# A decoder layer on one core: room for the gates' sources, scalings two by two, sums of down weights placed anew

## The chip, the cores and the metric

The kernel runs on one core of a Trainium2 chip. The metric is the device time of one execution in microseconds (us). Engines: PE (TensorE, matmuls), DVE (VectorE), ACT (ScalarE), POOL (GpSimd) and SP (SyncE, which only issues DMAs here).

## The reference, cut to what matters

One layer of a decoder with 2048 prompt tokens and 64 sample tokens (2112 in all), width 1024, in float32:

```python
h = rms_norm(x, pre_mix_g)
q, k, v, sg_u, sg_v, mq, gate_logits = split(h @ w_in)
# three branches of width 512: window attention, spatial gating, attention into 256 memory rows
sg = u * (tril(sg_w) @ layer_norm(gelu(sg_v)) + sg_b)        # u = gelu(sg_u)
gates = sigmoid(gate_logits)                                 # 3 x 1024 columns
mixed = sum over branches n of gates[n] * (branch[n] @ w_o[n])
x = x + rms_norm(mixed, post_mix_g)
up = rms_norm(x, pre_ffn_g) @ w_up                           # 5632 columns
c = conv_b + three shifted rows of up * conv_w               # causal convolution along tokens
act = gelu(gate half of c) * value half of c                 # 2816 columns
x = x + rms_norm(act @ w_down, post_ffn_g)
```

Outputs are x for prompt and sample tokens, and the caches (keys, values, memory keys and values, the layer-normed sg_v of the samples, the last rows of up).

## The kernel before, in words

Everything is transposed: features on the 128 partitions, tokens along the free axis. A float32 product is made of three passes (`PASSES`): each operand is split into a high part (a cast on ACT, L76) and a low part (a subtraction on DVE, L77), and high by high, high by low and low by high are added in PSUM.

Stage 1 walks over pairs of 128-token blocks. Its first pass (`pass_a`) makes queries, keys, values and both attentions; its weights are five units, `w_a`. Its second pass (`pass_b`) makes the spatial gating with four units, `w_b` (products sv and up, the masked product into psg at L732, then the bias L736 and the product by uT at L737, which gives the branch rows ob, stored at L739). Units are tiles of the pool `w1` (five tiles of 16 KB a partition), loaded in halves through the staging pool `st1` (`load_w1`). Beside them stand `h1`, `st1`, `live1` (values that live through a pair: scores, qT, vg, uT) and `small`. The second pass also prepares sums for the up weights with f < 14: `prep_sums` loads four blocks of a weight, forms four sums or differences on DVE, splits each and stores it to `sum_d`; its tiles are in `raw1b` (5) and `wo1b` (2), on the right side of SBUF.

Stage 2 takes the tokens in three groups of T2 = 704 (two chunks of CW = 352). Its first phase makes the gates (12 weight blocks), its third the up product (22 blocks f), both by one level of Strassen's scheme: a job is one block for one group, seven products of 12 matmuls with sums of the weights (`weights`, L821 raw loads, L847 loads of prepared sums) and sums of the activations (`operands`: load L778, scaling by gain and row norm L780, differences L790, seven sets of four operand tiles). The gates' x and their differences are in the pool `ldg` on the right side (eight tiles of x, one of the norm, four half tiles of differences, 11 × T2 × 4 bytes), the raw weights in `rawg`, next to it. `p5`, `u2` and the like are copies of PSUM tiles on ACT (L891); the sums of products are evicted on DVE (`Sink.add`).

The mix phase takes each group through the three branches n and four blocks op of w_o. A step (n, op) has two tiles o of 24 matmuls (L1023); each is multiplied by its gate (L1032 for n = 0, which makes m; L1035 for the others, then added on POOL, L1036). When a group is done, its rows m, with the sum of their squares, are held, and `post_mix` of the held group runs inside the next group, after the step (n, op) = (0, 1): the row norm, then for each of the eight tiles o a load of x, a scaling of m (L1000, DVE), the addition of x (L1003, POOL), the store of x1 and its square. The last group has no next group in the mix; `late` does the same for it in the up phase, one tile at a time after the blocks f = 2 to 9 of group 0.

In the up phase the jobs are written in the order of g and f. After the blocks f = 3, 7, 11, 15, 19 of group 0 and 3, 7, 11 of group 1 stands a `prep_sums` for one of the eight down weights, d0 to d7. After f = 14 stands `norms`, the row norm of the next group; the next group's operands follow the last block. The up and down phases share a ring of weight tiles, `wof`, with 11 tiles.

The down phase works with two Strassen blocks b and a plain remainder for each group; `final` then scales a group's eight tiles y (L1306), adds x1 (L1310, loaded at L1304 into two tiles) and stores them (L1311). Groups 0 and 1 do that inside the next group's first products; the next group's first product is copied into a y tile at L1229, and such a tile is free when its old y has been stored. In the last group the two chunks are finished one after the other, and in the very last one the odd tiles are added on POOL.

The program is not executed in the order in which it is written. A planner places each engine's instructions, in the order of the program among those that it takes to be ready at that time by its own costs. On the engine the order is then fixed. A pool's tile may lie where an earlier, closed pool's tiles lay (`reuse_waits="tile"`); then its first write waits for the last use of just those tiles that it overlaps. SP issues all loads and stores in one queue.

Of the kernel before, what the change touches and what calls it, by code (L numbers as in the profile page):

```python
# [15 lines left out]
P = 128  # L16
# [114 lines left out]
def stage1(tc, I, O, br, rbc_d, mhalf, gains, split, PASSES, rstd_rows, ident, ident_r, prep_sums, sum_d):  # L131
    nc = tc.nc
    PSUM = bass.MemoryType.PSUM
    with ExitStack() as c1:
        wp = c1.enter_context(tc.tile_pool(name="w1", bufs=5))
        hp = c1.enter_context(tc.tile_pool(name="h1", bufs=3))
        st = c1.enter_context(tc.tile_pool(name="st1", bufs=3))
        lv = c1.enter_context(tc.tile_pool(name="live1", bufs=2))
        small = c1.enter_context(tc.tile_pool(name="small", bufs=2))
        ps_mm = c1.enter_context(tc.tile_pool(name="ps_mm", bufs=3, space=PSUM))  # L140
        ps_o = c1.enter_context(tc.tile_pool(name="ps_o", bufs=1, space=PSUM))
        ps_tr = c1.enter_context(tc.tile_pool(name="ps_tr", bufs=2, space=PSUM))

        def load_w1(u, stage=None, before=None):
            w = wp.tile([P, 2, KT * 256], F32R, tag="w", name=f"w1_{u}")
            for i in range(2):
                if before:
                    before(i)
                t = stage(f"ws_{u}_{i}") if stage else st.tile([P, 1024], F32, tag="st", name=f"ws_{u}_{i}")
                nc.sync.dma_start(out=t, in_=I["w1"][u][:, i * 1024 : (i + 1) * 1024])  # L150
                split(w[:, 0, i * 1024 : (i + 1) * 1024], w[:, 1, i * 1024 : (i + 1) * 1024], t)
            return w
# [97 lines left out]
        sample = ("s", NP, NS, None)  # L250
        with ExitStack() as c2:
            kc = c2.enter_context(tc.tile_pool(name="const1", bufs=1, side="right"))
            wk = c2.enter_context(tc.tile_pool(name="work1", bufs=2, side="right"))
            pass_a(pairs[:2] + [sample] + pairs[2:], dict(locals()))
        with ExitStack() as c2:
            wk = c2.enter_context(tc.tile_pool(name="work1b", bufs=2, reuse_waits="tile"))
            rw = c2.enter_context(tc.tile_pool(name="raw1b", bufs=5, side="right", reuse_waits="tile"))
            wo = c2.enter_context(tc.tile_pool(name="wo1b", bufs=2, side="right", reuse_waits="tile"))
            pass_b(pairs[:1] + [sample] + pairs[1:], dict(locals()))


def pass_a(items, a):
# [41 lines left out]
    rb_mem, r_mem = rstd_of(x_mem, NMEM, "mem")  # L304
    w_a = [load_w1(4 + u, stage) for u in range(5)]
    band = kload("band", [P, 256])
# [597 lines left out]
def gate_phase(c2, tc, env):  # L904
# [4 lines left out]
    lp, rw = pool(c2, "ldg", 1, "right"), pool(c2, "rawg", 11, "right")  # L909
    cp, gp = pool(c2, "cpg", 7), pool(c2, "sg", 4)  # L910
    op_ = {n: pool(c2, "g" + n, 4) for n in ("t4", "b21", "t1", "b11", "t3", "b22", "t2")}
    wo = pool(c2, "wog", 12)
    eng = Strassen(ps2, op_, wo, rw, cp, lp)
# [33 lines left out]
def mix_phase(c2, tc, env):  # L947
# [11 lines left out]
    spare.tile([P, 3456], F32, tag="spare", name="spare")  # L959
    bc, sp, wp, gp, me = (pool(c2, nm, n) for nm, n in (("bc", 4), ("s2", 2), ("w2", 3), ("sg2", 5), ("mxe", 8)))  # L960
    hp = ba, bb, bc
# [26 lines left out]
    def post_mix(g, mx, acc):  # L988
# [5 lines left out]
        nc.vector.tensor_copy(out=v2(rs), in_=psb[:, :, :CW])  # L994
        acx = xp.tile([P, T2], F32, tag="ax", name=f"acx_{g}")
        for o in range(KT):
            m = mx[o]
# [6 lines left out]
            nc.sync.dma_start(out=x1_d[g][o], in_=m)  # L1004
            square(acx, m, o == 0, f"x{g}_{o}")
        nc.sync.dma_start(out=acx_d[g], in_=acx)

    held = None
    for g in range(NG2):
        mx = []  # L1010
        acc = sp.tile([P, T2], F32, tag="ac", name=f"ac_{g}")
        for n in range(3):
            bs = load_br(g, n)
            for op in range(4):
                w = load_w(I["wp"][4 * n + op], f"p{g}_{n}_{op}")
                for oo in range(2):
# [20 lines left out]
                    if n == 2:  # L1037
                        square(acc, mx[o], o == 0, f"m{g}_{o}")
                        if g + 1 == NG2:
                            nc.sync.dma_start(out=m_d[o], in_=mx[o])  # L1040
                if held and n == 0 and op == 1:
                    post_mix(*held)
                    held = None
        held = g, mx, acc
    nc.sync.dma_start(out=acm_d, in_=acc)


def ffn_phase(c2, tc, env):

    pool = env["pool"]  # L1050
    env["lp"], env["rw"], env["wo"] = (
        pool(c2, nm, n, "right") for nm, n in (("ldf", 1), ("rawf", 5), ("wof", 11))
    )
    env["op_"] = {n: pool(c2, "f" + n, 4, "right") for n in ("b11", "t1")}
    env["op_"].update({n: pool(c2, "f" + n, 4) for n in ("b21", "t2", "b22", "t3", "t4")})
    for phase in (up_phase, down_phase):
        with ExitStack() as c3:
            phase(c3, tc, env)


def up_phase(c2, tc, env):
# [127 lines left out]

    def jobs():  # L1190
        ops, rs = ops0, None
        for g in range(NG2):
            for f in range(NF):
                yield f"u{g}_{f}", eng.weights(I["w3"][f], sum_d[f], False, f"u{g}_{f}"), ops, Sink(g, f)
                if f % 4 == 3 and 5 * g + f // 4 < 8:
                    i = 5 * g + f // 4
                    prep_sums(rw, wo, I["w4s"][i], sum_d[NF + 12 + i], f"d{i}")
                if g == 0 and 2 <= f < 2 + KT:
                    rs = rs or norms(acm_d, "m")
                    late(f - 2, rs)  # L1200
                if f == 14 and g + 1 < NG2:
                    rb = norms(acx_d[g + 1], str(g + 1))
# [7 lines left out]
def down_phase(c2, tc, env):  # L1210
# [84 lines left out]
    def final(g, ys, acc, cs):  # L1295
# [6 lines left out]
        for o in range(KT):  # L1302
            x = sp.tile([P, T2], F32, tag="x", name=f"xf_{g}_{o}_{c0}", bufs=2)
            nc.sync.dma_start(out=x[:, c0:c1], in_=x1_d[g][o][:, c0:c1])  # L1304
# [166 lines left out]
```

## Time and profile before

| | us |
|---|---|
| median of three runs | 3004.3 (3001.31 to 3009.29) |
| the profiled execution | 3005.72 |
| span of its profile | 3003.9 |
| PE busy | 2876.0 (96%) |
| DVE busy | 2064.8 (69%) |
| ACT busy | 1397.5 (47%) |
| POOL busy | 488.3 (16%) |

The span is the time between the first and the last event that the profile shows. Matmuls are pipelined, and a busy PE isn't always PE at its full rate; the column PEclk of a window is the clock that was granted, as a share of full speed. In a timeline a row gives the start, the time, the engine, the line, the operation with output and input, and in brackets the idle time before it with what ended that. Several like instructions in a row are one row with their count.

### The profile page before, as it was taken

The page shows a single profiled execution, that of the slowest core. Times are in us where ns is not written, and L with a number is a line of the kernel's source. Part 1 is how long each engine was busy: PE and PEld are TensorE (multiplying, and loading weights), DVE is VectorE, ACT ScalarE, POOL GpSimd, SP SyncE. Part 2 cuts the span into 40 slices and gives each one's busy share as a digit, 9 for nine tenths or more (in the row PEclk, how much of TensorE's full clock was granted, in tenths as well). Part 3 has the DMA queues.
Part 4 walks back from the last instruction along what each step waited for, and adds up shares of the span by engine and source line. Part 5 has one row for each costly group of instructions (what it writes and reads, how often), then busy time and mean ns, then how long its engine had stood idle before and what let it go on. Part 6 is the DMA issues. An engine that isn't in the chain of part 4 may idle for free. (4 is left out here: it accounts for less than half of the span.)

```text
span 3003.9 us, 52626 instructions
## 1 busy us (share of the span) xinstructions
PE 2876.0 (96%) x19340; PEld 2829.2 (94%) x19340; DVE 2064.8 (69%) x3901; ACT 1397.5 (47%) x2799; POOL 488.3 (16%) x576
## 2 busy tenths in 40 slices
PE   8999999996999999999999899999999999999996
PEld 8998999996999999999989899999999999999996
DVE  6676567888867363478798677766775667667665
ACT  5555557333555353432235355644554454343332
POOL 3221100010000000035453121311231121000000
PEclk9999999998999999999999899999999999999998
DMA  6222224787989999867669788887777778576673
GB/s 209 53 69 85 76 68 126 258 303 248 328 296 371 332 356 346 320 212 264 212 249 364 291 304 310 319 288 278 246 277 247 240 238 279 196 273 223 233 246 119
DMA packets 310946, 732.33 MB, mean 244 GB/s; under 512 B 37968, under 2 KB 90192, under 8 KB 310672
## 3 DMA queue, kind: packets, MB, share of 16 engines
q1 hardware_dynamic: 310688, 728.97, 69.9%
q8 instruction: 153, 2.51, 0.3%
q14 instruction: 105, 0.86, 0.1%
HBM read 553.55 MB, written 176.27 MB: 243 GB/s over the span
## 5 line engine op out<-in xcount | busy, mean ns | idle before, releaser
L1023 PE MATMUL ps_p<-b,w_p 128*128 128x352 f32 x1728 | 287.2, 328 | 13.3 <-DVE m L1032 8.8
L1023 PEld LDWEIGHTS ps_p<-b,w_p 128*128 128x128 f32 x1728 | 283.3, 192 | 15.1 <-issue 10.2
L1165 DVE SCALAR_TENSOR_TENSOR c<-e,k_conv_w,c 128x704 f32<-128x704 f32 (+1 forms) x264 | 251.6, 954 | 43.3 <-ACT c L1161 36.0
L882 PE MATMUL ps_xu<-ot_u,ws_u 128*128 128x352 f32 x1584 | 274.9, 322 | 0.0
L882 PEld LDWEIGHTS ps_xu<-ot_u,ws_u 128*128 128x128 f32 x1584 | 257.1, 188 | 0.0
L1036 POOL TENSOR_TENSOR m<-m,sl 128x704 f32<-128x704 f32 x48 | 101.4, 2119 | 658.0 <-DVE sl L1035 651.8
L77 DVE TENSOR_TENSOR wa_u<-r_u,wa_u 128x512 fp32r<-128x512 f32 x198 | 138.6, 703 | 48.0 <-ACT wa_u L76 43.9
L1161 ACT ACTIVATE c<-e,k_conv_b,k_conv_w 128x704 f32<-128x704 f32 (+1 forms) x132 | 129.6, 981 | 78.6 <-DVE e L1140 43.5
L882 PE MATMUL ps_xu<-ob_u,wa_u 128*128 128x352 f32 x792 | 149.0, 325 | 9.7 <-ACT wa_u L76 9.7
L1152 POOL COPY tails<-e 128x2 f32<-128x2 f32 x88 | 79.2, 900 | 470.0 <-DVE e L1140 469.6
L882 PE MATMUL ps_xg<-ot_h,ws_g 128*128 128x352 f32 x864 | 151.1, 323 | 1.7 <-ACT ws_g L76 0.8
L882 PE MATMUL ps_wu<-ob_u,wa_u 128*128 128x352 f32 x792 | 147.0, 324 | 1.1 <-DVE ob_u L77 1.1
L882 PE MATMUL ps_yu<-ot_u,ws_u 128*128 128x352 f32 x792 | 143.2, 325 | 3.8 <-DVE sl L1035 2.2
L76 ACT CAST wa_u<-r_u 128x512 fp32r<-128x512 f32 x198 | 123.1, 623 | 47.1 <-PE ps_xu L882 15.7
L882 PEld LDWEIGHTS ps_xg<-ot_h,ws_g 128*128 128x128 f32 x864 | 140.6, 188 | 2.4 <-ACT ws_g L76 1.3
L882 PEld LDWEIGHTS ps_xu<-ob_u,wa_u 128*128 128x128 f32 x792 | 131.7, 190 | 9.9 <-ACT wa_u L76 9.9
L1279 PE MATMUL ps_p<-a,wd 128*128 128x352 f32 x864 | 140.1, 323 | 0.0
L1279 PEld LDWEIGHTS ps_p<-a,wd 128*128 128x128 f32 x864 | 138.4, 188 | 0.1
L882 PE MATMUL ps_xu<-ot_u,wa_u 128*128 128x352 f32 x792 | 138.0, 323 | 0.0
L882 PE MATMUL ps_yu<-ob_u,ws_u 128*128 128x352 f32 x792 | 137.7, 323 | 0.0
L882 PEld LDWEIGHTS ps_yu<-ot_u,ws_u 128*128 128x128 f32 x792 | 130.9, 190 | 4.6 <-DVE sl L1035 2.5
L1140 DVE TENSOR_TENSOR e<-p_u,ps_wu 128x352 f32<-128x352 f32 x66 | 34.3, 519 | 145.1 <-PE ps_wu L882 140.3
(381 smaller groups left out, 6786.2 us busy)
## 6 DMA issues: line engine op xcount, KB each, us to landing
ws_u<-sum_d SPq DMA_DIRECT2D x264, 512.0 KB, 4.9
r_u<-in_w_dram SPq DMA_DIRECT2D x286, 256.0 KB, 4.7
ws_g<-sum_d SPq DMA_DIRECT2D x96, 512.0 KB, 8.5
ws_d<-sum_d SPq DMA_DIRECT2D x96, 512.0 KB, 5.1
sum_d<-ws_u SPq DMA_DIRECT2D x88, 512.0 KB, 4.2
r_g<-in_wg_dram SPq DMA_DIRECT2D x120, 256.0 KB, 5.3
r_d<-in_w4s_dram SPq DMA_DIRECT2D x104, 256.0 KB, 4.4
sg_d<-sg SPq DMA_DIRECT2D x72, 352.0 KB, 5.0
```

The source lines that it names most:

```text
L76: nc.scalar.copy(out=hi, in_=src)
L77: nc.vector.tensor_tensor(out=lo, in0=src, in1=_f(hi), op=ALU.subtract)
L882: nc.tensor.matmul(ps[:, :CW], lhsT=ws[w][:, a, j], rhs=ops[o][j][:, b], start=(start and n == 0), stop=(n == 3 * HK - 1), skip_group_chec ...
L1023: nc.tensor.matmul(ps[:, c, :CW], lhsT=w[:, a, 4 * oo + k], rhs=bs[k][:, b, c * CW : (c + 1) * CW], start=(i == 0), stop=(i == 11),)
L1036: nc.gpsimd.tensor_tensor(out=mx[o], in0=mx[o], in1=sg, op=ALU.add)
L1140: lambda out, part: nc.vector.tensor_tensor(out=out, in0=part(p), in1=part(q), op=ALU.add), h, c
L1152: nc.gpsimd.tensor_copy(out=tails[:, ft], in_=e[:, T2 : T2 + 2])
L1161: nc.scalar.activation(c[:, :cwid], e[:, 2:ew], AF.Identity, bias=cb[:, ft : ft + 1], scale=cw[:, ft, 2:3])
L1165: nc.vector.scalar_tensor_tensor(out=c[:, :cwid], in0=e[:, t : t + cwid], scalar=cw[:, ft, t : t + 1], in1=c[:, :cwid], op0=ALU.mult, op1= ...
L1279: nc.tensor.matmul(ps[:, :CW], lhsT=w[k // 4][:, a, k % 4], rhs=acts[k][c][:, b], start=(n == 0), stop=(n == 3 * ND - 1),)
```

## The change

Four things change in where tiles lie and when instructions are written; what is computed stays the same.

1. Stage 1: `w1` has four tiles and not five; the first unit of `w_a` gets a pool of its own, `w1x`, on the right side, in the first pass only. `small` stands before `live1`. In the second pass a pool `free1b` of 11 × T2 × 4 bytes is laid on the right side before `raw1b` and `wo1b`, and nothing uses it. In the gate phase the pools of operands and weights are opened in another order.
2. Mix: `post_mix` is a generator that stops after the row norm and after every second tile; the loop resumes it after each step from (0, 1) on.
3. Up phase: the eight preps of down weights stand after the blocks named in `preps`; the next group's norm stands after f = 18. The ring `wof` has 10 tiles.
4. `final`: x has four tiles, and for the last group eight tiles of the pool that held the operands' x.

```diff
-        wp = c1.enter_context(tc.tile_pool(name="w1", bufs=5))
+        wp = c1.enter_context(tc.tile_pool(name="w1", bufs=4))
         hp = c1.enter_context(tc.tile_pool(name="h1", bufs=3))
         st = c1.enter_context(tc.tile_pool(name="st1", bufs=3))
+        small = c1.enter_context(tc.tile_pool(name="small", bufs=2))
         lv = c1.enter_context(tc.tile_pool(name="live1", bufs=2))
-        small = c1.enter_context(tc.tile_pool(name="small", bufs=2))
...
         with ExitStack() as c2:
+            wx = c2.enter_context(tc.tile_pool(name="w1x", bufs=1, side="right"))
...
             wk = c2.enter_context(tc.tile_pool(name="work1b", bufs=2, reuse_waits="tile"))
+            free = c2.enter_context(tc.tile_pool(name="free1b", bufs=1, side="right", reuse_waits="tile"))
+            free.tile([P, 11 * T2], F32, tag="free", name="free1b")
...
-    w_a = [load_w1(4 + u, stage) for u in range(5)]
+    w_a = [load_w1(4 + u, stage, pool=None if u else a["wx"]) for u in range(5)]
...
-    cp, gp = pool(c2, "cpg", 7), pool(c2, "sg", 4)
-    op_ = {n: pool(c2, "g" + n, 4) for n in ("t4", "b21", "t1", "b11", "t3", "b22", "t2")}
-    wo = pool(c2, "wog", 12)
+    op_ = {n: pool(c2, "g" + n, 4) for n in ("b21", "t1", "b11", "t4")}
+    wo, cp, gp = pool(c2, "wog", 12), pool(c2, "cpg", 7), pool(c2, "sg", 4)
+    op_.update({n: pool(c2, "g" + n, 4) for n in ("t3", "b22", "t2")})
...
-    bc, sp, wp, gp, me = (pool(c2, nm, n) for nm, n in (("bc", 4), ("s2", 2), ("w2", 3), ("sg2", 5), ("mxe", 8)))
+    wp, bc, sp, gp, me = (pool(c2, nm, n) for nm, n in (("w2", 3), ("bc", 4), ("s2", 2), ("sg2", 5), ("mxe", 8)))
...
         acx = xp.tile([P, T2], F32, tag="ax", name=f"acx_{g}")
+        yield
         for o in range(KT):
...
             square(acx, m, o == 0, f"x{g}_{o}")
+            if o % 2:
+                yield
...
-                if held and n == 0 and op == 1:
-                    post_mix(*held)
-                    held = None
-        held = g, mx, acc
+                if held and (n, op) > (0, 0):
+                    next(held, None)
+        held = post_mix(g, mx, acc)
...
-        pool(c2, nm, n, "right") for nm, n in (("ldf", 1), ("rawf", 5), ("wof", 11))
+        pool(c2, nm, n, "right") for nm, n in (("ldf", 1), ("rawf", 5), ("wof", 10))
...
+        preps = [(g, f) for g, fs in ((0, (11, 14)), (1, (2, 5, 8, 11, 14)), (2, (2,))) for f in fs]
...
-                if f % 4 == 3 and 5 * g + f // 4 < 8:
-                    i = 5 * g + f // 4
+                if (g, f) in preps:
+                    i = preps.index((g, f))
...
-                if f == 14 and g + 1 < NG2:
+                if f == 18 and g + 1 < NG2:
...
-            x = sp.tile([P, T2], F32, tag="x", name=f"xf_{g}_{o}_{c0}", bufs=2)
+            if g + 1 == NG2:
+                x = lp.tile([P, T2], F32, tag="ld", name=f"xf_{g}_{o}_{c0}", bufs=8)
+            else:
+                x = sp.tile([P, T2], F32, tag="x", name=f"xf_{g}_{o}_{c0}", bufs=4)
```

## Rows read from the trace of the kernel before

**Rows 1.** The page, busy times of the engines: busy us, share, instructions.

```profile
PE 2876.0 (96%) x19340; PEld 2829.2 (94%) x19340; DVE 2064.8 (69%) x3901; ACT 1397.5 (47%) x2799; POOL 488.3 (16%) x576
```

**Rows 2.** The waits of PE: line and tile, releaser, total us, times, longest us.

```profile
PE ps_xg L882 <- ACT wa_g L76: 19.1, 2, 17.0
PE ps_xd L882 <- ACT y L1229: 17.5, 3, 6.8
```

**Rows 3.** Windows: length, busy us of PE, PEld, DVE, ACT, POOL, clock, DMA.

```profile
690.00:715.00 25.00, 25.00 (x212) 25.00 (x211) 20.45 (x34) 9.08 (x19) 2.25 (x4) 1.00 0.84 295
...
724.00:764.00 40.00, 14.31 (x56) 12.33 (x54) 40.00 (x74) 17.65 (x39) 0.00 (x0) 0.62 0.55 179
1381.00:1392.00 11.00, 6.56 (x26) 6.55 (x26) 11.00 (x11) 3.20 (x4) 5.28 (x3) 0.69 0.66 194
...
1680.00:1702.00 22.00, 9.84 (x35) 9.14 (x36) 17.16 (x27) 3.98 (x7) 0.78 (x1) 0.53 0.72 248
1800.00:1900.00 100.00, 100.00 (x626) 100.00 (x626) 77.60 (x126) 60.17 (x114) 26.59 (x29) 1.00 0.85 302
2671.00:2683.00 12.00, 5.20 (x25) 4.91 (x24) 9.65 (x15) 2.64 (x7) 0.00 (x0) 0.72 0.69 231
```

**Rows 4.** The timeline, end of stage 1 to the gates.

```profile
715.61 5.52 SPq L778 DMA_DIRECT2D x_h<-in_xT_dram  x8
...
721.67 1.81 DVE L780 SCALAR_TENSOR_TENSOR x_h<-x_h,c_gains,rb 128x704 f32<-128x704 f32 x2 [2.52 <-DMA x_h<-in_xT_dram]
...
743.00 0.68 DVE L737 TENSOR_TENSOR ob<-ob,uT_p 128x512 f32<-128x512 f32 x1
...
744.14 1.50 SPq L821 DMA_DIRECT2D r_g<-in_wg_dram  x3
```

**Rows 5.** The page, costliest groups: count, busy us, mean ns, idle before: POOL's adds.

```profile
L1036 POOL TENSOR_TENSOR m<-m,sl 128x704 f32<-128x704 f32 x48 | 101.4, 2119 | 658.0 <-DVE sl L1035 651.8
```

**Rows 6.** The timeline of DVE in the mix.

```profile
1371.73 12.81 DVE L1000 SCALAR_TENSOR_TENSOR m<-m,c_gains,rs 128x704 f32<-128x704 f32 x8
```

**Rows 7.** Line 1000, the scalings of the mix: ns least, median, most.

```profile
L1000 DVE SCALAR_TENSOR_TENSOR m<-m,c_gains,rs x16: 939/1653/2432, 1371.7 to 1484.7; 128x704 f32<-128x704 f32 x16
```

**Rows 8.** The timeline, early in the up stage.

```profile
1683.90 6.12 DVE L780 SCALAR_TENSOR_TENSOR x_u<-x_u,c_gains,rb 128x704 f32<-128x704 f32 x7
...
1691.09 0.62 ACT L76 CAST ws_d<-s_d 128x512 fp32r<-128x512 f32 x1 [10.01 <-DVE s_d L113]
```

**Rows 9.** The timeline of DVE in the middle of the up stage.

```profile
2101.10 0.68 DVE L77 TENSOR_TENSOR wa_u<-r_u,wa_u 128x512 fp32r<-128x512 f32 x1
2101.70 4.39 DVE L780 SCALAR_TENSOR_TENSOR x_u<-x_u,c_gains,rb 128x704 f32<-128x704 f32 x5
```

**Rows 10.** The timeline, a middle scaling of the down stage.

```profile
2667.48 6.99 DVE L1306 SCALAR_TENSOR_TENSOR y<-y,c_gains,rs_d 128x704 f32<-128x704 f32 x8
...
2674.39 1.69 DVE L1310 TENSOR_TENSOR y<-y,xf 128x704 f32<-128x704 f32 x2
...
2677.86 0.45 ACT L1229 COPY y<-ps_xd 128x352 f32<-128x352 f32 x1 [5.77 <-DMA out_yT_dram<-y]
```

**Rows 11.** The timeline, the end of the kernel.

```profile
2982.24 4.72 DVE L1306 SCALAR_TENSOR_TENSOR y<-y,c_gains,rs_d 128x352 f32<-128x352 f32 x8
...
3000.25 0.92 POOL L1310 TENSOR_TENSOR y<-y,xf 128x352 f32<-128x352 f32 x1 [3.44 <-DMA xf<-x_d]
3001.20 0.33 SPq L1311 DMA_DIRECT2D out_yT_dram<-y  x1
```

**Rows 12.** The timeline, from stage 1's first pass to its second.

```profile
461.18 0.39 SPq L156 DMA_DIRECT2D x_bp<-in_xT_dram  x1
...
465.69 2.00 ACT L76 CAST w<-ws 128x1024 fp32r<-128x1024 f32 x2
...
472.06 0.40 PE L215 MATMUL ps_sv<-w,h_bp 128*128 128x256 f32 x2
```

**Rows 13.** The page, DMA issues: count, KB, median us to landing: the prepared sums.

```profile
ws_u<-sum_d SPq DMA_DIRECT2D x264, 512.0 KB, 4.9
```

More of the change, by code (lines that the diff above doesn't have):

```diff
@@ L142, in stage1, with load_w1 @@
         ps_tr = c1.enter_context(tc.tile_pool(name="ps_tr", bufs=2, space=PSUM))
-        def load_w1(u, stage=None, before=None):
-            w = wp.tile([P, 2, KT * 256], F32R, tag="w", name=f"w1_{u}")
+        def load_w1(u, stage=None, before=None, pool=None):
+            w = (pool or wp).tile([P, 2, KT * 256], F32R, tag="w", name=f"w1_{u}")
             for i in range(2):
```

## The prediction

> **What bounds the kernel now.** First I read the busy times: PE works 2876.0 us of a span of 3003.9, 96% [rows 1]. So the change can only win where PE waits, or in the tail. Next come the waits of PE: the longest are for a weight cast at the entry of the gates (17.0 us) and for the y copy in the down stage (6.8) [rows 2]. Then the windows give each loss its size. An undisturbed stretch runs 626 matmuls in 100 us at a granted clock of 1.00, so 0.16 us each; the reader is to take a window's length less its matmuls times 0.16 as what was lost there, lower clock included [rows 3]. That gives: entry of the gates 40 − 56 × 0.16 = 31.0 us (clock 0.62, DVE busy all 40.00 us); the scalings of the mix 11 − 26 × 0.16 = 6.8, and a second burst of the same kind, for the next group, some 100 us later; the early up stage 22 − 35 × 0.16 = 16.4 (clock 0.53); a scaling in the middle of the down stage 12 − 25 × 0.16 = 8.0, again one of two [rows 3]. Last the timeline around each window shows what came late [rows 4, 6, 8, 10 to 12].
>
> The profiled execution took 3005.72 us, 1.8 over its span and 1.4 over the median of 3004.3. I sum against 3005.72 and take off 1.4 at the end. A measurement of this kernel can tell some 0.3% (9 us) from no change.
>
> **Entry of the gates.** The eight loads of the gates' x are issued at 715.61, because their pool lies over the raw and sum tiles of the second pass, and the first scaling runs at 721.67; the last branch product reads uT at 743.00, and the gates' raw weights, whose pool lies over uT's, are issued at 744.14 [rows 4]. After the change `free1b` (11 × 704 × 4 bytes, the size of the gates' x pool) keeps that place untouched in the second pass, so loads and scalings can run during it. The raw weights' pool then lies over `raw1b` and `wo1b`, which are done before uT is. DVE has room: 20.45 us busy of the 25 before 715 [rows 3]. Eight scalings and the first four differences can go ahead. What can't: the operand tiles now lie over stage 1's weights and live tiles, in use to about 724. That leaves 12 differences and 28 low parts, and 4 sums and 7 low parts for the first job's weights, 51 instructions of DVE. At the window's mean, 40.00 / 74 = 0.54 us [rows 3], they take 27.5 us, while the first job keeps PE busy for 84 × 0.16 = 13.4. So 14.1 us of loss stay; I allow one more and take 15, a gain of 31 − 15 = 16. Bounds: 27, if the lower parts arrive in the order in which PE eats them, and 5, if the three operand tiles over the live ones wait for the last product as the weights do now.
>
> **Mix.** The eight scalings of the held group run in a row for 12.81 us [rows 6], and the m eviction that PE waits for stands behind them. Now they come two by two after the steps (n, op) = (0, 2), (0, 3), (1, 0) and (1, 1): two scalings (2 × 1.65 us, the median [rows 7]) lie beside a step of 48 matmuls, 7.7 us, and PE has three PSUM tiles of 3.8 us to go on with. The planner puts an earlier instruction between later ones where it is ready: at 2101.10 a low part sits between the third and fourth of eight scalings [rows 9]. The two bursts lose 2 × 6.8 = 13.6; I take 9, bounds 0 and 13.6. The norm stays at (0, 1); the scalings move, and with each pair its two x loads, two adds on POOL, two squares and two x1 stores, later by one to four steps (8 to 31 us); no instruction of the mix reads that x1. The x loads stand between the slice loads on SP's queue two at a time, which I cost at nothing, because a step has 7.7 us for them.
>
> A scaling takes 1653 ns in the median and 939 at the least in the same form [rows 7], and what runs beside it is POOL's adds, of which the mix has 48 of its own, 2119 ns each, from n = 1 on, where the last four scalings now lie [rows 5]. The Trainium skill, page "SBUF — State Buffer", section "🔬 SBUF: two separate sides", says that DVE with two SBUF inputs and GpSimd reading SBUF share one port pair as an exclusive lock, held for the whole instruction by whoever came first. The rows agree so far as the scaling is slower beside POOL; by that rule the spreading saves no DVE time and puts half of it where POOL is busier, and the mix would win nothing.
>
> **Early up stage.** The sums d0 and d1 of the down weights are prepared at f = 3 and 7, beside the late x1 of the last group; seven scalings hold DVE for 6.12 us from 1683.90, the sum s_d comes behind them, ACT's cast of it idles 10.01 us, and the weight cast that PE needs stands behind that on ACT [rows 8]. With the preps at (0, 11), (0, 14), five in group 1 and one in group 2, no sum lies on ACT's queue there, and the norm for group 1 moves from f = 14 to 18. The scalings come anyway; a low part gets in between them [rows 9]. I take 13 of the 16.4, bounds 0 and 16.4. The later preps stand beside undisturbed jobs, where DVE has 77.60 busy of 100 us and ACT 60.17 [rows 3], at nothing. Without that cover one prep (4 sums and 4 low parts) holds DVE for 8 × 0.54 = 4.3 us, eight of them for 35; if a tenth of that fell on the path, it would cost 3.5, which lies within the upper bound of the layouts below.
>
> **Tail.** After the last scalings (2982.24 + 4.72 = 2986.96) the adds wait for x, which comes two tiles at a time, and the last add runs at 3000.25 and the last store is issued at 3001.20 [rows 11]. With eight x tiles of the `ld` pool all are there: last add to 2987.9 on POOL (0.92), store issued 0.33 us, then the 2.4 that stand between 3001.53 and the end of the span, in all 2990.6, 13.3 earlier. Eight stores at 0.33 us on SP's queue may keep 2 of it: 11, bounds 9 and 13.
>
> **Middle scalings of the down stage.** x gets 4 tiles for 2. But DVE does all eight scalings first (6.99 us), then adds at once without a wait for x, and the copy that PE waits for needs the first y out [rows 10]. More x tiles don't bring the first store earlier: 0, bounds +4 (four loads more on SP's queue before the weights) and −16 (two times 8.0).
>
> **Second pass of stage 1.** The weights have 4 tiles for 5, so each unit takes the place of a unit that is used one later. Now the first x is issued at 461.18, the last unit's cast runs at 465.69, and the first matmul at 472.06 [rows 12]. I charge one unit's lateness as the 6.4 us from cast to matmul: +6, bounds 0 and +14 (the 10.9 us from x to matmul and some of the lower clock behind it).
>
> **The up and down stages' weights.** The ring goes from 11 tiles to 10. A job takes 7, one per product of 12 × 0.16 = 1.93 us; a tile is wanted again 9 products later, 17.4 us, and a load lands in 4.9 us [rows 13]. So 0; with the other layouts −5 to +8.
>
> **Sum.** −16 − 9 − 13 − 11 + 0 + 6 + 0 = −43. 3005.7 − 43 = 2962.7, on the median 2961. Added as independent distances (the root of the sum of squares, the middle scalings' −16 left to rival B), the bounds reach 23 up and 15 down: this case's own range is 2946 to 2984.
>
> **Rivals.**
> B: with four x tiles the adds get in between the scalings and the first y goes out at once, so both middle stalls go: 2961 − 16 = 2945. For it: the adds stand earlier in the program than the later scalings. Against: x was there already and DVE still did eight scalings first [rows 10].
> C: the scalings of the mix stay at 1.65 us or more beside POOL's adds and the evictions still wait: the 9 stay lost, 2970. For it the median against the least [rows 7]; against it, that two of them fit into a step. It is what the rule of the Trainium skill's page on SBUF gives.
> D: the stalls are replaced. The entry of the gates wins its lower bound, 5, because DVE, busy all 40 us there [rows 3], stays behind; mix 0; half of the up stage, 6.5; tail 11; second pass +6: −16.5, 2988.
> E: the same with the lower bounds everywhere, within 9 us of 3004.
> F, slower: the ring of 10. If a tile came free so late that PE waited in each of 66 up and 24 down jobs, the change decides against itself from 43 / 90 = 0.48 us a job, and 0.6 us would give 3004 − 43 + 54 = 3015. Against it: 17.4 us stand against 4.9. For it: a prep takes 4 tiles of the ring at once, and 6 are left, 11.6 us.
>
> **How the numbers follow.** Forecast 0.38, B 0.17, C 0.10, D 0.18, E 0.08, F 0.09. The time is the forecast's, 2961. The range runs from 2930 (B with the better half of the bounds) to 2992 (D and a little), and leaves out E, F and a little of B and D. Faster by over 0.3%: A to D, 0.83; the same 0.08; slower 0.09.
>
> **What would show it.** In the profile after: x_h issued before 700 and the wait for the gates' first weight cast under 5 us; scalings of the mix in twos and no wait of PE on m over 1 us; no PE gap over 3 us when the scalings of the second up group run; the last add ending within 2 us of the last scaling, and the span within 5 us of it; the middle waits for the y copy still at 6.8; PE waiting some 6 us, between the two passes of stage 1, for a cast of the second pass's weights or of its x. Wrong would be a PE gap that moved with its size to another line, or an interval over 0.16 us per matmul in 1800 to 1900.

## The result and the profile after

The changed kernel takes 2973.4 us in the median of four runs (2970.51 to 2977.45), against 3002.81 of the kernel before in the same count: a ratio of 0.9899, 95% interval 0.9882 to 0.9916, so 29 us or 1.0% faster. The profiled execution took 2972.76 us, its span 2970.9. The forecast was 2961, range 2930 to 2992: the sign and the range held, the gain was two thirds of the 43 us. Two of the places that the sum named gave theirs, the early up stage and the tail; the other two, the entry of the gates and the mix, gave nothing; and some 14 us came from places that it had at nothing. One of the ten executions of the run *w1 only* below took 11797.26 us; of the other nine the median is 2995.91.

The page of the changed kernel, busy times, to set against [rows 1]:

```profile
PE 2868.4 (97%) x19340; PEld 2821.0 (95%) x19340; DVE 2057.4 (69%) x3901; ACT 1395.8 (47%) x2793; POOL 499.2 (17%) x576
```

Its waits of PE (line and tile, releaser, us in total, times, longest), against [rows 2]. The wait for the gates' weight cast is still there, and longer; the one for the up stage's weight cast, the last row here and from the kernel before, is gone; the middle one of the down stage has a new releaser:

```profile
PE ps_xg L885 <- ACT wa_g L76: 20.6, 2, 18.3
PE ps_xd L885 <- DVE wa_d L77: 11.6, 3, 5.3
PE ps_p L1029 <- DVE m L1038: 9.0, 2, 4.5
```

```profile
PE ps_xu L882 <- ACT wa_u L76: 9.7, 1, 9.7
```

Its windows, moved to the same work as in [rows 3] (length, busy us of PE, PEld, DVE, ACT and POOL with counts, clock, DMA share, GB/s):

```profile
520.00:548.00 28.00, 26.07 (x219) 25.35 (x218) 22.38 (x37) 7.63 (x14) 0.78 (x2) 1.00 0.90 286
680.00:705.00 25.00, 25.00 (x212) 25.00 (x211) 19.18 (x32) 7.89 (x16) 2.25 (x4) 1.00 0.84 289
713.00:753.00 40.00, 11.61 (x45) 9.99 (x43) 37.24 (x70) 17.85 (x41) 0.00 (x0) 0.62 0.75 264
1376.00:1387.00 11.00, 6.48 (x29) 6.44 (x29) 11.00 (x10) 3.20 (x4) 5.60 (x3) 0.69 0.67 200
...
1655.00:1677.00 22.00, 22.00 (x141) 21.99 (x140) 13.00 (x19) 10.12 (x18) 4.20 (x8) 1.00 1.03 406
...
2644.00:2656.00 12.00, 6.13 (x20) 5.67 (x21) 10.66 (x16) 2.81 (x6) 0.00 (x0) 0.66 0.64 196
```

The early up stage runs at full rate now. The entry of the gates and the mix are no better than they were. And a stall that the forecast had not named is gone: in the kernel before the samples' work in the second pass of stage 1 held 148 matmuls in 28 us at a clock of 0.76, now 219 at 1.00:

```profile
528.00:556.00 28.00, 23.07 (x148) 22.36 (x147) 20.94 (x39) 7.62 (x14) 0.78 (x2) 0.76 0.77 252
```

To see where the time went in every kernel I cut each trace at the same matmuls (the last up product of the second pass, the 168th matmul of the gates, and so on) and added, for each stretch, PE's idle time and half of its busy time at the lower granted clock (half of full speed). The mix is cut inside its third group, so the column *into up* begins with the last part of the mix. Each row is one profiled execution. In us lost:

| kernel | to second pass | second pass | entry of gates | rest of gates | mix | into up | up | into down | middle scalings, down | tail |
|---|---|---|---|---|---|---|---|---|---|---|
| before | 16.6 | 13.8 | 31.1 | 9.3 | 14.2 | 8.9 | 18.3 | 6.3 | 22.7 | 22.5 |
| changed | 18.2 | 2.4 | 34.6 | 8.7 | 13.5 | 8.2 | 0.0 | 3.7 | 25.5 | 12.8 |
| preps back | 17.0 | 2.4 | 36.2 | 9.2 | 13.9 | 10.1 | 20.1 | 12.0 | 23.0 | 12.8 |
| norm back | 18.2 | 1.4 | 33.0 | 8.8 | 13.8 | 9.9 | 0.0 | 13.2 | 25.2 | 12.8 |
| no free1b | 18.0 | 10.2 | 26.4 | 9.3 | 12.5 | 8.2 | 0.0 | 3.7 | 25.7 | 12.9 |
| final back | 16.9 | 4.2 | 34.8 | 8.7 | 13.9 | 10.1 | 0.0 | 5.0 | 25.4 | 21.9 |
| twelve | 18.4 | 5.3 | 11.5 | 26.5 | 12.2 | 8.0 | 0.0 | 3.7 | 25.6 | 12.8 |
| spread | 17.5 | 1.3 | 33.8 | 9.9 | 4.5 | 11.9 | 0.0 | 12.9 | 25.0 | 12.8 |
| w1 only | 17.9 | 8.8 | 26.0 | 8.6 | 12.2 | 9.1 | 19.1 | 5.6 | 23.8 | 22.0 |
| all at once | 17.7 | 3.6 | 35.8 | 9.3 | 12.4 | 8.9 | 0.0 | 5.3 | 25.6 | 12.8 |
| twelve, even | 16.9 | 5.1 | 10.0 | 16.9 | 15.0 | 8.6 | 0.0 | 3.7 | 25.6 | 12.8 |
| spread, order | 17.8 | 2.0 | 37.6 | 9.6 | 4.5 | 18.6 | 0.0 | 5.0 | 23.3 | 12.8 |
| all three | 18.3 | 1.4 | 9.5 | 14.8 | 4.8 | 15.7 | 0.0 | 4.3 | 24.6 | 12.8 |
| k2 first | 18.7 | 1.1 | 9.8 | 20.0 | 4.4 | 12.2 | 0.0 | 10.4 | 23.4 | 12.9 |

From before to changed these losses fall by 36.1 us and the span by 33.0; the 3 us between them, and up to 12 in other pairs of rows (from *before* to *all three* the losses fall by 57.5 and the span by 45.4), I have not placed. Differences of 1 to 2 us in a cell come and go without a cause in the edit.

### The profile page after: what moved, and what is told of

Read it like the earlier page. It is cut to its first block, busy times and chain, and to the rows that moved or that the text cites. A ratio compares the mean times of both kernels' runs of the same rounds, so it can differ in the third digit from the quotient of the medians.

```text
span 2970.9 us, 52583 instructions
## 1 busy us (share of the span) xinstructions
PE 2868.4 (97%) x19340; PEld 2821.0 (95%) x19340; DVE 2057.4 (69%) x3901; ACT 1395.8 (47%) x2793; POOL 499.2 (17%) x576
## 4 chain that ended last, share of the span: by engine, by line
PE 87%; DVE 4%; DMA 4%; issue 2%; ACT 2%; POOL 1%; SPq 0%; DVEq 0%; ACTq 0%; POOLq 0%
PE ps_xu L885 17%; PE ps_xg L885 9%; PE ps_yu L885 9%; PE ps_p L1029 8%; PE ps_xd L885 6%; PE ps_yg L885 5%; PE ps_p L1285 5%; PE ps_wu L885 4%; PE ps_q L215 3%; PE ps_yd L885 3%; PE ps_mqp L229 3%; PE ps_wg L885 2%; PE ps_kv L215 2%; PE ps_sv L215 2%; PE ps_wd L885 1%
## 5 line engine op out<-in xcount | busy, mean ns | idle before, releaser
L1157 POOL COPY tails<-e 128x2 f32<-128x2 f32 x88 | 71.5, 813 | 456.5 <-DVE e L1145 446.4
L885 PEld LDWEIGHTS ps_wu<-ob_u,wa_u 128*128 128x128 f32 x792 | 130.3, 188 | 0.0
```

The costliest lines, as they stand in the source:

```text
L885: nc.tensor.matmul(ps[:, :CW], lhsT=ws[w][:, a, j], rhs=ops[o][j][:, b], start=(start and n == 0), stop=(n == 3 * HK - 1), skip_group_chec ...
L1157: nc.gpsimd.tensor_copy(out=tails[:, ft], in_=e[:, T2 : T2 + 2])
```

## The experiments

Times are medians beside the kernel before on the same chip (its medians there run from 3003.34 to 3004.39); after each stands the ratio to it with its 95% interval (the changed kernel: 0.9899, 0.9882 to 0.9916).

**The preps back.** In the changed kernel:

```diff
-                if (g, f) in preps:
-                    i = preps.index((g, f))
+                if f % 4 == 3 and 5 * g + f // 4 < 8:
+                    i = 5 * g + f // 4
```

> The changed kernel with the eight preps of the down weights back after f = 3, 7, 11, ... (the norm stays at f = 18). Theory: the preps d0 and d1 beside the late x1 made the loss early in the up stage (16 to 18 us), so it comes back in that stage: about 2973 + 17 = 2990 us, with a PE gap of over 5 us before a weight cast. Rival: the norm of the next group, moved to f = 18, is what helped; then the stage stays without a gap and the time within 5 us of 2973.

2999.46 us (0.9984, 0.9974 to 0.9994). The up stage lost 20.1 us again. Its timeline shows the chain of [rows 8] whole: the cast of a sum waits 11.66 us on ACT for DVE, and PE 12.38 for the weight cast behind it:

```profile
1688.65 0.62 ACT L76 CAST ws_d<-s_d 128x512 fp32r<-128x512 f32 x1 [11.66 <-DVE s_d L113]
1689.18 1.13 ACT L76 CAST wa_u<-r_u 128x512 fp32r<-128x512 f32 x2
1689.84 0.50 PEld L885 LDWEIGHTS ps_xu<-ob_u,wa_u 128*128 128x128 f32 x2 [12.54 <-ACT wa_u L76]
1689.85 0.95 PE L885 MATMUL ps_xu<-ob_u,wa_u 128*128 128x352 f32 x2 [12.38 <-ACT wa_u L76]
```

The norm stood at f = 18 here and didn't help. Another 8 us were lost on the way into the down stage (12.0 against 3.7), on which more below; with them the time is 9 over the 2990 of the theory.

**The norm back.**

```diff
-                if f == 18 and g + 1 < NG2:
+                if f == 14 and g + 1 < NG2:
```

> The changed kernel with the norm of the next group back at f = 14 (the preps stay where the change put them). Theory: the preps alone decide, so no gap comes back and the time stays within 5 us of 2973. Rival: the norm's place decides; the gap comes back and the time is about 2990 us.

2979.69 us (0.9910, 0.9888 to 0.9933; single runs from 2967.74 to 2982.13). No gap in the up stage: the preps alone made that gain. The profiled execution took 2981.2, 8.4 over that of the changed kernel, and the entry of the down stage lost 13.2 against 3.7: ACT idles 8.49 us before a y copy there, until the store of the last activation has landed, as in the spread run below. In the changed kernel the scalings of group 1 are still eight in a row, but late and with no cast of a sum on ACT's queue beside them, and PE has no gap there:

```profile
1823.39 6.99 DVE L783 SCALAR_TENSOR_TENSOR x_u<-x_u,c_gains,rb 128x704 f32<-128x704 f32 x8
```

**Without the room.** The changed kernel without `free1b`:

```diff
-            free = c2.enter_context(tc.tile_pool(name="free1b", ...
-            free.tile([P, 11 * T2], F32, tag="free", name="free1b")
```

> The changed kernel without the pool free1b, so that the preps' tiles lie at the right edge again and the gates' x loads have to wait for them. Theory: at the entry of the gates the raw weights, which wait for the last preps, end last, not the x; so it costs only what the 8 scalings and 4 differences (9.7 us of DVE) put on the path behind the last preps, 3 to 10 us: 2976 to 2983. Rival: early x is worth the whole of the first forecast and the loss at the entry is hidden elsewhere: over 2986. The second rival: the room itself is what delayed the preps; then the entry gets better and the time is under 2970.

2971.26 us (0.9891, 0.9877 to 0.9906). All three theories missed: the room costs 8.2 us at the entry of the gates (34.6 against 26.4) and is paid back by 7.8 in the second pass (2.4 against 10.2). So the second rival was right that the entry gets better and wrong about the time. Its queue shows why. Without the room the raw weights are the early ones, the first seven issued between 532 and 547, and x is the late one:

```profile
532.29 1.72 SPq L822 DMA_DIRECT2D r_g<-in_wg_dram  x2
...
720.11 5.01 SPq L779 DMA_DIRECT2D x_h<-in_xT_dram  x8
```

In the changed kernel it is the other way round (below). So `free1b` brought x forward and sent the raw weights back behind the preps.

**The final scalings back**, to two x tiles everywhere:

```diff
-            if g + 1 == NG2:
-                x = lp.tile([P, T2], F32, tag="ld", name=f"xf_{g}_{o}_{c0}", bufs=8)
-            else:
-                x = sp.tile([P, T2], F32, tag="x", name=f"xf_{g}_{o}_{c0}", bufs=4)
+            x = sp.tile([P, T2], F32, tag="x", name=f"xf_{g}_{o}_{c0}", bufs=2)
```

> The changed kernel with two x tiles in every final scaling, as before. Theory: the tail is 9 to 11 us longer again, the middle scalings keep their loss of some 8 to 10 us each whatever the number of x tiles: 2973 + 10 = 2983. Rival: the four x tiles in the middle scalings shortened them too, or the moved loads were bought there: the middle losses would change by over 4 us each.

2984.99 us (0.9934, 0.9919 to 0.9949): 11.6 over the changed kernel, 9.1 of it in the tail, the middle the same (25.4 and 25.5). The theory holds.

**Twelve preps in the second pass.**

```diff
-NF1 = 14
+NF1 = 12
...
-                if g and i % 3 == 0:
+                if g and (i % 3 == 0 or i == 1):
```

> The changed kernel with 12 and not 14 preps of up weights in the second pass of stage 1; the other two go to the gate phase with the eight that are there. Theory: the gates' first raw weights are issued only when the last prep's sums are stored, 14 us after PE has done the pass; with the preps over before the pass ends they are issued some 15 us earlier against the end of the pass, and of the 34.6 us lost at the entry 10 to 18 come back: about 2960 us. Rival: DVE, which has the operands, the last branch products and the first job's weights to do, bounds the entry; the raw weights come earlier and PE waits as long, for DVE: within 5 us of 2973.

2971.89 us (0.9894, 0.9880 to 0.9909): by time the rival is right, and still the theory of the entry is shown: 34.6 fell to 11.5. The changed kernel's timeline has x early, and the raw weights behind the last stores of sums (an x load of the next group, which waited 2.6 us for DVE, stands between them):

```profile
530.75 0.90 SPq L781 DMA_DIRECT2D x_h<-in_xT_dram  x2
```

```profile
731.92 0.92 SPq L116 DMA_DIRECT2D sum_d<-ws_u  x2
...
735.58 0.33 SPq L781 DMA_DIRECT2D x_h<-in_xT_dram  x1
...
735.96 1.37 SPq L824 DMA_DIRECT2D r_g<-in_wg_dram  x3
...
740.35 0.96 PE L885 MATMUL ps_xg<-ob_h,wa_g 128*128 128x352 f32 x2 [18.25 <-ACT wa_g L76]
```

With twelve preps the same queue issues them at 710.24, again right behind the last sums, and that is before the pass ends (its last up product begins at 717.03); x is issued from 531.88, so here both sources are early:

```profile
708.08 2.11 SPq L116 DMA_DIRECT2D sum_d<-ws_u  x2
710.24 4.29 SPq L824 DMA_DIRECT2D r_g<-in_wg_dram  x7
```

Of the 23.1 us, 17.8 were lost again in the rest of the gates (26.5 against 8.7) and 2.9 in the second pass. The gates' loss shows as two gaps of 4.6 and 8.9 us before a weight cast; that the new prep after job 1, beside the making of operands, makes them is argued. Windows of this run, entry first:

```profile
717.00:757.00 40.00, 34.26 (x180) 32.50 (x179) 39.12 (x75) 26.50 (x57) 0.00 (x0) 0.83 0.71 248
945.00:965.00 20.00, 14.87 (x78) 14.12 (x77) 8.33 (x14) 8.58 (x15) 0.00 (x0) 0.83 0.85 290
1092.00:1114.00 22.00, 12.47 (x60) 11.82 (x59) 11.52 (x18) 9.63 (x18) 0.00 (x0) 0.77 0.93 336
```

**The scalings really spread**, by a ring of two tiles that POOL's add frees:

```diff
-    spare.tile([P, 3456], F32, tag="spare", name="spare")
+    spare.tile([P, 2048], F32, tag="spare", name="spare")
...
+            t = xp.tile([P, T2], F32, tag="t", name=f"xt_{g}_{o}", bufs=2)
...
-                out=m, in0=m, scalar=gains[:, 2, o : o + 1], in1=rs, op0=ALU.mult, op1=ALU.mult
+                out=t, in0=m, scalar=gains[:, 2, o : o + 1], in1=rs, op0=ALU.mult, op1=ALU.mult
...
-            nc.gpsimd.tensor_tensor(out=m, in0=m, in1=x, op=ALU.add)
+            nc.gpsimd.tensor_tensor(out=m, in0=t, in1=x, op=ALU.add)
```

> The changed kernel with the scaling of the mix written into a ring of two tiles t, which POOL's add reads, so that a scaling has to wait for the add two places before it and can't be placed ahead; the room is taken from the unused spare tile. Theory: the generator didn't move the scalings because the planner places whatever is ready; once they are really spread, the m evictions get between them and the two gaps of 4.5 us (6.8 us each with the lower clock) go: about 2960 us. Rival: DVE is blocked by POOL's adds as long as they run beside each other, so the scalings hold up the evictions wherever they lie: gaps of the same sum, within 4 us of 2973.

2974.89 us (0.9906, 0.9891 to 0.9920): no gain in time, but the two waits for m are gone, and up to the cut in its third group the mix lost 4.5 for 13.5. DVE's timeline in the changed kernel, and then in this run; the scalings are L1004 and L1005, the evictions L1038 and L1039:

```profile
1366.86 12.78 DVE L1004 SCALAR_TENSOR_TENSOR m<-m,c_gains,rs 128x704 f32<-128x704 f32 x8
1379.57 0.87 DVE L1038 TENSOR_TENSOR m<-sl,ps_p 128x704 f32<-128x704 f32 x1
```

```profile
1364.30 1.81 DVE L1005 SCALAR_TENSOR_TENSOR xt<-m,c_gains,rs 128x704 f32<-128x704 f32 x2
1366.03 0.88 DVE L1039 TENSOR_TENSOR m<-sl,ps_p 128x704 f32<-128x704 f32 x1
1367.02 1.78 DVE L77 TENSOR_TENSOR w_p<-ws_p,w_p 128x1024 fp32r<-128x1024 f32 x1
1368.72 3.29 DVE L1005 SCALAR_TENSOR_TENSOR xt<-m,c_gains,rs 128x704 f32<-128x704 f32 x2
1371.93 0.88 DVE L1039 TENSOR_TENSOR m<-sl,ps_p 128x704 f32<-128x704 f32 x1
```

The 9 us went in two places: 3.7 in the column *into up*, and 9.2 at the entry of the down stage. The 3.7 are still the mix's own: its last part, after the cut, loses 7.7 for 2.2, with longer waits for sl, the products scaled by their gate, while from the last matmul of the mix on the up stage loses 4.3 for 6.0. First the changed kernel, then this run:

```profile
PE ps_p L1029 <- DVE sl L1041: 2.2, 2, 1.6
```

```profile
PE ps_p L1030 <- DVE sl L1042: 6.8, 3, 4.0
```

The entry of the down stage shows a y copy that waits for the last activation's store to land:

```profile
2470.46 0.33 SPq L1194 DMA_DIRECT2D act_d<-e  x1
...
2477.47 0.81 ACT L1236 COPY y<-ps_xd 128x352 f32<-128x352 f32 x2 [8.13 <-DMA act_d<-e]
...
2478.33 3.01 PE L885 MATMUL ps_xd<-ot_d,ws_d 128*128 128x352 f32 x9 [4.71 <-ACT y L1236]
```

**All at once**: the stops taken out, so that one resumption runs all eight.

```diff
-        yield
         for o in range(KT):
...
-            if o % 2:
+            if o == 99:
                 yield
```

> The changed kernel with all eight scalings written at one place again, after the step (0, 1). Theory: the places in the program don't bind the planner, so that the eight run in one row with or without the stops, and the time stays within 4 us of 2973 with the two gaps of 4.5 us unchanged. Rival: the stops did spread something that pays (the adds, the squares or the stores): 5 us or more slower.

2977.36 us (0.9905, 0.9886 to 0.9924; runs from 2968.73). The mix lost 12.4, its gaps were 4.52 and 4.61, and the eight ran in one row of 12.78 us as they do with the stops. So the stops moved no scaling out of that row on DVE. The median is at the edge of what was expected, within the spread of the runs.

**The weight tiles alone.** The kernel before, with four tiles in `w1` and the pool `w1x` for the first unit, as in the change.

```diff
-        wp = c1.enter_context(tc.tile_pool(name="w1", bufs=5))
+        wp = c1.enter_context(tc.tile_pool(name="w1", bufs=4))
...
+            wx = c2.enter_context(tc.tile_pool(name="w1x", bufs=1, side="right"))
```

> The kernel before with one part of the change, the four weight tiles of stage 1 and the pool for the first unit. Theory: it moves the first matmul of the second pass some 5 us back, and nothing else; the stall of PE at the samples' gelu in the second pass (11.8 us with the lower clock) stays, because the order of ACT's work there comes from the preps and the early x: about 3003 + 4 = 3007 us. Rival: the later weights are what put the samples' work into another order; the stall goes and the time is about 2994 us.

2995.99 us (0.9973, 0.9963 to 0.9983). The theory fell, and by time the rival is nearer: the second pass lost 8.8 against 13.8, though its stall didn't go whole, and the entry of the gates 26.0 against 31.1. Here too the raw weights are issued early, from 531.95, and x at 718.97: four weight tiles alone free the raw weights' place. The cost that was feared (into the second pass) was 1.3.

**Three fixes.** Twelve preps with the ten others after even jobs (*twelve, even*); the spread with the up stage's pools in another order (*spread, order*); both (*all three*); and with a third order of the pools, k2, cp, e2 (*k2 first*).

```diff
-                if g and i % 3 == 0:
+                if g and i and i % 2 == 0:
...
-    kp, ep, cp = pool(c2, "k2", 1), pool(c2, "e2", 6), pool(c2, "cp", 7)
+    cp, kp, ep = pool(c2, "cp", 7), pool(c2, "k2", 1), pool(c2, "e2", 6)
```

> The changed kernel with 12 preps of up weights in the second pass, and the ten others in the gate phase after the jobs 2, 4, 6, 8 and 10 of the second and third group, away from the jobs in which that group's operands are made. Theory: the entry of the gates keeps the 23 us that the run with twelve won there, and the 18 us which that run lost later in the gates (gaps of 4.6 and 8.9 us before a weight cast, a prep beside the operands) don't come: 2973 - 23 = 2950 us, or a little less. Rival: ten preps are too many for the gates' rings wherever they lie; the gates lose 10 us or more again and the time is over 2960.

2965.41 us (0.9871, 0.9858 to 0.9885). The entry keeps its gain (10.0 lost), and the rest of the gates loses 16.9 and not 26.5, where the changed kernel lost 8.7: half of what the theory wanted, and the rival's 10 us are nearly there. The time falls by 8.

> The changed kernel with the scalings really spread (the ring of two tiles t) and the up stage's pools opened in another order, cp, k2, e2, so that the first y tiles of the down stage no longer lie on the tile from which the last activation is stored (its store takes some 7 us to land). Theory: the spread run won 9 us in the mix and lost 9 again at the entry of the down stage, because its y copy waited for that store; with the order of the pools that wait goes: down entry under 5 us lost, and 2973 - 9 + 2 (the entry of the up stage) = 2966 us. Rival: the wait comes from somewhere else, the down entry still loses over 9 us, and the time stays at 2973 to 2975.

2977.91 us (0.9918, 0.9905 to 0.9932). The down entry came back to 5.0, as the theory of the y tiles says, but the column *into up* went from 11.9 to 18.6, all of it after the mix's last matmul (4.3 to 10.7), and the time missed the theory's 2966 by 12.

> The changed kernel with all three: twelve preps in the second pass and ten at even jobs of the gates, the scalings spread by the ring t, the pools of the up stage in the other order. Theory: the three places are apart, so the gains add: 2973 - 23 - 7 = 2943 us. Rival: what is won at one place is lost at the next, as with the run with twelve and the first spread; then it is within 5 us of the better of the two runs beside it.

2963.22 us (0.9864, 0.9851 to 0.9878): 9.5 at the entry of the gates, 4.8 in the mix, 4.3 into the down stage, but 14.8 in the rest of the gates and 15.7 into the up stage. By time the rival is right: it is within 5 us of the better of the two beside it.

> As the run with all three, but with the up stage's pools in the order k2, cp, e2, so that the copies cp of the up stage's first job don't lie lowest, where the mix's last tiles were. Theory: the 5 to 10 us that the other order lost at the entry of the up stage (15.7 and 18.6 us lost there against 8.2 in the changed kernel and 11.9 with the spread alone) come from where cp lies; the entry loses under 13 us, the down entry stays under 6, and the time is 2963 - 4 = 2959 us. Rival: the loss comes from the mix's last evictions, which the spread pushed back; the entry stays at 15 us or more and the time within 3 us of 2963.

2963.04 us (0.9856, 0.9840 to 0.9872). The column *into up* fell to 12.2, below the 13 of the theory (from the mix's last matmul on 4.4, after 9.0 in *all three*), and the down entry rose to 10.4: one lottery for the other. These last two are the fastest versions, 40 us under the kernel before and 10 under the changed one.

## Why the prediction was right, and where it was not

**Entry of the gates, −16 forecast, +3.5 measured.** The failed step reads: "The raw weights' pool then lies over `raw1b` and `wo1b`, which are done before uT is." They are done after it: in the changed kernel the last branch product reads uT at 729.30, the last sums are stored at 731.92, 19 us after the pass's last up product began (712.75), and the raw weights are issued at 735.96.

```profile
729.30 0.69 DVE L740 TENSOR_TENSOR ob<-ob,uT_p 128x512 f32<-128x512 f32 x1
```

What I had from the kernel before was preps over before the last branch product, and I took that order over. Without the room they are stored by 719.58; that the early x work beside them is what holds them up is argued, not shown. Early x itself came as forecast (530.75 instead of 715.61), but it was bought with late raw weights, and either alone leaves PE waiting for the other: 34.6 lost with early x, 26.4 and 26.0 with early raw weights, 11.5 and 10.0 with both, in the runs with twelve preps. The sum had left 15 for a kernel with both early, so that size was well judged. Those two runs also take the work of two preps off DVE; how much of their gain that is stays open.

**Mix, −9 forecast, −0.7 measured.** The failed step: that the scalings "come two by two" where they are written. On DVE they stay eight in a row (12.78 us), because none of them waits for anything once the norm is there, and the planner takes what is ready: without the stops the row is the same, with a ring that makes them wait it breaks up. The price of 9 was right for the two waits (9.0 us), but not for the stage: spread by a real wait, the whole mix lost only some 3.5 less, for the waits for sl grew by 4.6. Rival C, with the rule of the Trainium skill's page "SBUF — State Buffer", section "🔬 SBUF: two separate sides", gave 2970, near the time measured, but for another reason: nothing was spread. The spread run speaks for the rule so far as a run here can. Two scalings beside POOL's adds still come to 3.29 us against 1.81. The median of all 16 fell, first in the changed kernel and then spread:

```profile
L1004 DVE SCALAR_TENSOR_TENSOR m<-m,c_gains,rs x16: 939/1656/2415, 1366.9 to 1479.3; 128x704 f32<-128x704 f32 x16
```

```profile
L1005 DVE SCALAR_TENSOR_TENSOR xt<-m,c_gains,rs x16: 939/947/2423, 1364.3 to 1495.3; 128x704 f32<-128x704 f32 x16
```

But DVE's busy time over the whole kernel stayed (2057.4 and 2055.5 us), so what the scalings saved other instructions took. Against C speaks that no wait for m is left.

**Up stage, −13 forecast, −18.3 measured.** The mechanism was right, by the preps alone; the bound of 16.4 was the loss in a window of 22 us, and some of the stall lay outside it.

**Tail, −11 forecast, −9.7 measured.** The x tiles were all there and the last add ended 2.5 us after the last scaling. What is missing is the scalings themselves: 6.07 us beside four adds on POOL instead of 4.72 beside one ([rows 11]), and 4.72 again in the run with two x tiles. The rows of the changed kernel:

```profile
2958.85 6.07 DVE L1315 SCALAR_TENSOR_TENSOR y<-y,c_gains,rs_d 128x352 f32<-128x352 f32 x8
...
2961.24 7.10 SPq L1320 DMA_DIRECT2D out_yT_dram<-y  x8
...
2964.84 2.55 DVE L1319 TENSOR_TENSOR y<-y,xf 128x352 f32<-128x352 f32 x4
```

**Middle scalings, 0 forecast.** Right in size (25.5 against 22.7, and 25.4 with two tiles); DVE still does all eight first, and PE now waits for the low part queued behind them, not for y ([rows 10]):

```profile
2641.20 6.99 DVE L1315 SCALAR_TENSOR_TENSOR y<-y,c_gains,rs_d 128x704 f32<-128x704 f32 x8
...
2648.10 0.69 DVE L77 TENSOR_TENSOR wa_d<-r_d,wa_d 128x512 fp32r<-128x512 f32 x1
...
2648.84 3.31 PE L885 MATMUL ps_xd<-ob_d,wa_d 128*128 128x352 f32 x10 [5.32 <-DVE wa_d L77]
```

**Into the second pass, +6 forecast.** The first matmul came 5.3 later (477.36 against 472.06), but PE lost only 1.6: other work stood beside it.

**Layouts, 0 forecast, −11.4 in the second pass and −2.6 into the down stage.** The range of −5 to +8 was too narrow. That the total came out so near is in part luck: the entry and the mix missed by 19.5 and 8.3 us, and these 14 us and the 5 more of the up stage made up for most of it. Without the 14 the time would have been some 2987, still inside the range but outside the 2946 to 2984 of the sum's own bounds, and about what rival D gave (2988). In the second pass PE waited for the samples' gelu, which on ACT stood behind two casts, the later one a prep's that had itself waited for a store; in the changed kernel it is placed ahead of both. (ACT idles 1.8 us right before the gelu in both.) First the kernel before, then the changed one:

```profile
539.19 0.62 ACT L76 CAST ws_u<-s_u 128x512 fp32r<-128x512 f32 x1 [0.97 <-DMA sum_d<-ws_u]
541.59 0.65 ACT L241 ACTIVATE zt_us<-ps_us 64x256 f32<-64x256 f32 x2 [1.78 <-DVE s_u L113]
542.02 0.47 PE L246 MATMUL ps_tus<-ident,zt_us 64*128 64x64 f32 x2 [4.93 <-ACT zt_us L241]
```

```profile
535.24 1.05 ACT L76 CAST h_bp<-x_bp 128x1024 fp32r<-128x1024 f32 x1 [1.72 <-PE ps_us L215]
538.06 0.65 ACT L241 ACTIVATE zt_us<-ps_us 64x256 f32<-64x256 f32 x2 [1.77 <-DMA br<-ob]
538.49 0.34 PE L246 MATMUL ps_tus<-ident,zt_us 64*128 64x64 f32 x2 [1.93 <-ACT zt_us L241]
```

The weight tiles bring 5.0 of it alone, and taking `free1b` out gives 7.8 back. Why the planner changes that order with the layout stays open. Open too is which edit decides on which tile the last activation lies, and so the 4 to 13 us at the entry of the down stage; that the wait is for that tile's store the rows of the spread run show. The run with the norm back, which moves no pool, has the same wait, so a layout is not all that decides. Rival F, the ring of ten tiles, shows nowhere: the stretch that holds most of the up jobs lost 0.0.

## What to carry to other kernels

Where a planner orders the engines, moving a line need not move the instruction: the preps went where they were written (the first cast of a down sum runs at 1708.6 and not at 1603.8) and made the largest gain, the scalings stayed in one row. To spread work that is ready, give it a ring that makes it wait, and look in the trace whether it did. When a wait is removed by freeing one buffer, list everything else that the first instruction needs, and take the time of each from the kernel as it will be, not as it was; the room that brings one source forward can send another back. The runs that change nothing but a layout (no `free1b`, the weight tiles alone, the orders of the pools) moved the losses of single stages by 3 to 8 us, about the size of the terms that one sums; the range has to hold that.

## What was not expected of the hardware

The last activation's store in the spread run, issued at 2470.46, kept a y tile until 2477.47, 7 us, where the 22 stores of that form in the same run land in 3.1 us in the median. And the scalings at the end took 0.76 us each beside four adds on POOL and 0.59 beside one: POOL's help cost DVE over a quarter there.
